# An encoder layer with a mixture of experts on one core: another form of the router, other weight buffers, a written order of the weight queue, and a last block by columns

## The chip, the cores and the metric

The kernel runs on one core of one Trainium2 chip. A core has five engines with a program of their own each: TensorE (PE: matmuls; PEld: its weight loads), VectorE (DVE), ScalarE (ACT), GpSimd (POOL) and SyncE (SP, which here only issues DMAs). Sixteen DMA engines move data between HBM and the core's SBUF. What is measured is the device time in microseconds (us) of one execution, as a median over runs.

## What is computed

One layer of a bidirectional encoder over 256 tokens of width 2048, in fp32, and a last norm:

```python
mod = silu(c) @ ada_w + ada_b                    # [1, 6*2048]
sh1, sc1, g1, sh2, sc2, g2 = split(mod, 6)
h = modulate(rmsnorm(x, norm1_g), sh1, sc1)
x = x + g1 * mixer(h, ...)                       # attention + FFT branches, gates, w_out
h = modulate(rmsnorm(x, norm2_g), sh2, sc2)
x = x + g2 * hier_moe(h, ...)                    # 4 groups x 8 experts, best group, top 2 in it
return rmsnorm(x, final_g)

# hier_moe: router, then SwiGLU experts of width 512
g_probs = softmax(h @ wg_r + bg_r)               # 4 groups
sel = (h @ we_r + be_r)[:, best group]           # 8 experts of it
weights = g_top_p * softmax(top2(sel))
y = sum over the two experts of weight * (silu(h @ w_gate[e]) * (h @ w_up[e])) @ w_down[e]
```

## The kernel before

The work is two long stages. In the **mixer stage** weights come as tiles of 128 x 1024 fp32 (512 KB) through `load` (L101 to L104): a tile is taken from the pool `wp`, which has NW = 8 buffers, and SP issues its DMA. Of each matmul tile ACT makes a rounded high part (`hi`, L107) and DVE the rest (`lo`, L108), so a buffer comes free when `lo` is done, and TensorE runs three matmuls (high by high, high by low, low by high) in place of one fp32 matmul: 24 of 256 columns or 12 of 512 columns per tile. Beside these run 192 tiles of the modulation matrix `ada_w`, which DVE alone multiplies (`dot`, L215, and `mac`, L223). SP's queue is in order: a load that waits for its buffer holds everything behind it. The order of SP's instructions up to the output projection is the scheduler's; in the projection's loop (L618 to L633) it is written out (`manual_schedule`).

The last part of the mixer is that projection (`mow`): four column blocks `cb` of 512, eight tiles each. Between its tiles stand `ada` tiles (`ada_some`), and quarters of the first five expert blocks (`early_some`, 20 loads of 512 KB into NA = 5 slots). The input is loaded again as `x1` (2 MB, L563); its place in SBUF is where gated sums of the mixer lay, so the load waits for the last gate addition on POOL (L543). After the last tile eight `ada` loads are issued (`late`). `residual` (L600 to L602) adds each column block to `x1` and makes its sum of squares on ACT; `router_part` transposes the block on TensorE, copies it on ACT, and accumulates the router's 36 logits in `plg` with the router's weights as the stationary operand: 4 matmuls with 256 moving columns. An fp32 matmul shows as two records. The part of block `cb` runs in the loop after five tiles of the next block; that of block 3 runs after the loop.

Then the **router chain**: sum of squares (L649), reciprocal root (L150 to L156), a copy of the logits to SBUF (`lgs`, L647), matmuls with a selection matrix that turn them to tokens by 36 (L116, `m<-cst,lgs`), `lg` (L656), best group and best two experts, ranks by a matmul with a triangular matrix, a gather matrix (`gt`, L742 and L744), and the gather itself (`ph`, `hq`), all on tiny tiles. The late `ada` tiles' `mac`s run on DVE ahead of it.

In the **expert stage** 192 blocks of 2 MB (`exw`, L727) stream from HBM: 8 quads of four experts, each with 16 gate/up blocks and 8 down blocks. A block takes a slot of SBUF and holds it until TensorE has used it. Slots 0 to 4 hold the early blocks, slots 5 and 6 (`wxb`) and 7 (`wx4`, used once, after which `x2` takes its place) can be loaded when the mixer's buffers are closed. After that NX = 7 slots go round. The last quad has a tail: `pd`, gate, `po`, residual, squares, then the norm's scale and four output DMAs.

Of the kernel before, what the change touches and what calls it, by code (L numbers as in the profile page):

```python
# [27 lines left out]
C_ID, C_LT, C_ONE, C_SELR, C_IOTA, C_DESC, C_THR, C_END = 0, 128, 256, 384, 420, 452, 484, 492  # L28
# [4 lines left out]
def const_table():  # L33
# [5 lines left out]
    for j in range(2):  # L39
        t[64 * j + np.arange(36), C_SELR + np.arange(36)] = 1  # L40
# [17 lines left out]
def build(tc, A, out, dbg=None):  # L58
# [15 lines left out]
    wp, _wp = pool("wp", "right", bufs=NW)  # L74
# [14 lines left out]
    def s4(shape, s, dt=F32):  # L89
        return r0.tile(shape, dt, tag="s4", bufs=6, name=nm(s))  # L90
# [74 lines left out]
    c16 = cp.tile([16, P], F32, name="c16")  # L165
    vec = cp.tile([P, P], F32, name="vec")
    vecT = cp.tile([P, P], F32, name="vecT")
    condT = cp.tile([P, KC], F32, name="condT")
    wr = cp.tile([P, KC, 36], F32, name="wr")
    rb = cp.tile([1, 36], F32, name="rb")  # L170
# [18 lines left out]

    condR = xp.tile([P, D], F32, name="condR")  # L190
    for i in range(2):
        crow = wp.tile([P, 1024], F32, tag="w", name=nm("crow"))
# [212 lines left out]
    for i, c in ((0, 1024), (2, 512)):  # L405
        fr = wp.tile([P, 1024], F32, tag="w", name=nm("fr"))
# [77 lines left out]
    def attention(half):  # L484
# [50 lines left out]
    _ra.close()  # L535
    mt, _mt = pool("mt", "right")
# [26 lines left out]
    nc.sync.dma_start(x1, A["x"])  # L563
# [32 lines left out]
    def residual(cb, acs):  # L596
        c = slice(512 * cb, 512 * cb + 512)
        for tb in range(2):
# [3 lines left out]
            nc.scalar.activation(tmp, x1[:, tb, c], AF.Square, accum_out=ss2[:, tb, cb:cb + 1])  # L602

    def router_part(cb):
        for pr in range(2):
            px = mps()
            for i in range(2):
                kc = 4 * cb + 2 * pr + i
                for tb in range(2):
                    nc.tensor.transpose(px[:, T * i + P * tb:T * i + P * tb + P],  # L610
                                        x1[:, tb, kc * P:kc * P + P], ident)
            xt2 = s4([P, 2, T], "x1t")
            nc.scalar.copy(xt2, px.rearrange("p (a b) -> p a b", a=2))
            for i in range(2):
                kc = 4 * cb + 2 * pr + i
                mm(plg[64 * i:64 * i + 36, 0:T], wra[:, kc, :], xt2[:, i, :], kc < 2, kc >= KC - 2)

    with tc.manual_schedule(engines={nc.sync.engine}):  # L618
        for cb in range(4):
            acs = acc_tiles()  # L620
            for s in range(8):
                n_part(load(A["mow"][cb, s]), acs, mhf, mlf, 2 * s, s == 0, s == 7)
                i = 8 * cb + s
                early_some(max(0, i - 5) * 4 * NA // 26 - max(0, i - 6) * 4 * NA // 26)
                ada_some((i + 1) * PACE // 32 - i * PACE // 32)
                if s == 4 and cb:
                    router_part(cb - 1)
                if s == 4 and cb == 1:

                    nc.scalar.activation(warm, ones[:, 0:1], AF.Sqrt)  # L630
            if cb == 3:
                late = [ada_load() for _ in range(len(ada_q))]
            residual(cb, acs)  # L633
    router_part(3)
    show("x1", x1)
    _mt.close()
    _wp.close()

    wxb, _wxb = pool("wxb", reuse_waits="tile")
    rt, _rt2 = pool("rt2", "right")  # L640
# [3 lines left out]
    lgs = rt.tile([P, T], F32, name="lgs")  # L644
    nc.gpsimd.memset(lgs, 0.0)
    for i in range(2):
        nc.vector.tensor_copy(lgs[64 * i:64 * i + 36, :], plg[64 * i:64 * i + 36, 0:T])  # L647
# [173 lines left out]
    for go in late:  # L821
        go()
# [172 lines left out]
```

## Time and profile before

| | us |
|---|---|
| median of three runs | 1601.78 (1601.13 to 1602.49) |
| the profiled execution, its own time | 1598.41 |
| its span (first to last instruction) | 1596.6 |
| mixer stage, about 15 to 640 of the span | 625 |
| router chain and gather, about 640 to 671 | 31 |
| expert stream, about 671 to 1581 | 910 |
| tail, about 1581 to 1597 | 16 |

Over the whole span PE is busy 77%, DVE 43%, ACT 22%, POOL 3%, and the DMA engines 95% in SP's queue. These are means over stages with different limits, so each stage has to be read by itself: first which engine is busy all the time in it, then which wait ends last where none is.

### The profile page before, as it was taken

The numbers are of one execution on the slowest core, as the hardware profiler recorded it, in microseconds if no ns is written. First come the engines' busy times: TensorE is split into PE (matmuls) and PEld (weight loads), VectorE is DVE, ScalarE is ACT, GpSimd is POOL, SyncE is SP. The second block draws the span as 40 slices with busy tenths as digits, with TensorE's granted clock in tenths as the row PEclk, the third lists the DMA queues.
The fourth block names the chain that finished last, engine by engine and source line by source line (L and its number), as shares of the span: only waits on it lengthen the run. The fifth ranks groups of instructions, "written<-read, shape, count | busy, mean of one in ns | idle before, by whom it ended". The sixth has DMA issues, their size and how long they took to land.

```text
span 1596.6 us, 20401 instructions
## 1 busy us (share of the span) xinstructions
PE 1233.2 (77%) x8430; PEld 745.9 (47%) x8430; DVE 679.3 (43%) x946; ACT 349.7 (22%) x535; POOL 43.6 (3%) x40
## 2 busy tenths in 40 slices
PE   4999999999999899679657567667567566556755
PEld 3989999999899777325112112112112112111111
DVE  6989999798887966603003002002002002002002
ACT  3543355444555343112000000000000000000002
POOL 0000000300002100000000000000000000000001
PEclk9999999999999999799889779789779889777878
DMA  9999999899997899699999999999999999999996
GB/s 360 389 337 339 352 359 365 273 328 369 329 346 267 318 409 380 261 427 426 427 426 427 428 427 426 427 426 427 426 427 428 427 427 426 417 427 426 425 428 280
DMA packets 89229, 616.27 MB, mean 386 GB/s; under 512 B 10037, under 2 KB 10341, under 8 KB 64937
## 3 DMA queue, kind: packets, MB, share of 16 engines
q1 hardware_dynamic: 87700, 611.10, 95.2%
q10 hardware_dynamic: 1252, 3.48, 0.6%
q8 instruction: 68, 1.11, 0.3%
q0 software_dynamic: 176, 0.31, 0.1%
q14 instruction: 33, 0.26, 0.0%
HBM read 611.71 MB, written 2.10 MB: 384 GB/s over the span
## 4 chain that ended last, share of the span: by engine, by line
DMA 47%; PE 38%; DVE 5%; issue 1%; ACT 1%; POOL 0%; DVEq 0%; POOLq 0%; ACTq 0%
DMA w<-exw 45%; PE acc L116 23%; PE pd L116 3%; PE m L116 2%; PE ph L116 2%; PE pg L116 2%; PE pu L116 2%; DMA w<-ada 2%; DVE lo L108 1%; DVE ada L223 1%; PE po L116 1%; PE at_u L116 1%; PE pr L116 0%; DVE t L600 0%; PE sp L116 0%
## 5 line engine op out<-in xcount | busy, mean ns | idle before, releaser
L116 PE MATMUL pg<-w,hq 128*32 128x512 f32 x1024 | 185.0, 777 | 217.0 <-DMA w<-exw 217.0
L108 DVE TENSOR_TENSOR lo<-w,hi 128x1024 fp32r<-128x1024 f32 x192 | 239.5, 1253 | 42.6 <-ACT hi L107 37.8
L107 ACT CAST hi<-w 128x1024 fp32r<-128x1024 f32 x192 | 200.8, 1051 | 229.2 <-PE acc L116 179.5
L790 DVE TENSOR_TENSOR act<-act,pu 128x512 f32<-128x512 f32 x8 | 5.5, 688 | 526.2 <-PE pu L116 526.2
L116 PE MATMUL acc<-hh,hi 128*128 128x256 f32 x768 | 212.1, 280 | 0.6 <-ACT hi L107 0.6
L116 PE MATMUL acc<-hl,hi 128*128 128x256 f32 x768 | 211.3, 278 | 0.0
L116 PE MATMUL acc<-hh,lo 128*128 128x256 f32 x768 | 205.7, 279 | 2.2 <-DVE lo L108 2.1
L116 PEld LDWEIGHTS pg<-w,hq 128*32 128x32 f32 x1024 | 25.0, 118 | 363.1 <-DMA w<-exw 345.3
L116 PE MATMUL pu<-w,hq 128*32 128x512 f32 x1024 | 190.0, 793 | 0.0
L223 DVE SCALAR_TENSOR_TENSOR ada<-w,condT,ada 128x1024 f32<-128x1024 f32 x124 | 162.1, 1314 | 13.1 <-DMA w<-ada 12.2
L116 PE MATMUL pd<-w,aT 128*32 128x512 f32 x1024 | 132.2, 630 | 37.0 <-DMA w<-exw 35.5
L116 PEld LDWEIGHTS acc<-hh,hi 128*128 128x128 f32 x768 | 145.3, 189 | 2.1 <-ACT hi L107 1.4
L116 PEld LDWEIGHTS acc<-hl,hi 128*128 128x128 f32 x768 | 145.1, 189 | 0.3 <-issue 0.2
L786 ACT ACTIVATE act<-pg 128x512 f32<-128x512 f32 x8 | 4.8, 597 | 637.3 <-PE pg L116 637.3
L116 PEld LDWEIGHTS acc<-hh,lo 128*128 128x128 f32 x768 | 141.2, 189 | 3.0 <-DVE lo L108 2.6
L116 PE MATMUL po<-yb,gwt 128*128 128x512 f32 (+1 forms) x132 | 75.0, 659 | 30.4 <-DVE yb L808 19.4
L116 PEld LDWEIGHTS pu<-w,hq 128*32 128x32 f32 x1024 | 43.0, 138 | 109.9 <-issue 108.2
L116 PEld LDWEIGHTS ph<-gt,x 128*128 128x128 f32 x512 | 65.2, 195 | 43.8 <-issue 25.6
L116 PEld LDWEIGHTS pd<-w,aT 128*32 128x32 f32 x1024 | 28.7, 112 | 114.7 <-issue 60.4
L215 DVE SCALAR_TENSOR_TENSOR w<-w,condR 128x1024 f32<-128x1024 f32 x64 | 77.7, 1219 | 9.1 <-ACT condR L197 7.4
L116 PE MATMUL ph<-gt,x 128*128 128x128 f32 x512 | 74.8, 288 | 7.1 <-ACT hq L756 3.5
L815 DVE TENSOR_TENSOR x<-x,po 128x512 f32<-128x512 f32 (+1 forms) x66 | 44.3, 671 | 79.8 <-PE po L116 79.8
(246 smaller groups left out, 1481.4 us busy)
## 6 DMA issues: line engine op xcount, KB each, us to landing
w<-exw SPq DMA_DIRECT2D x186, 2048.0 KB, 30.7
w<-ada SPq DMA_DIRECT2D x192, 512.0 KB, 5.8
w<-mixw SPq DMA_DIRECT2D x64, 512.0 KB, 5.6
w<-gatew SPq DMA_DIRECT2D x64, 512.0 KB, 5.4
w<-mow SPq DMA_DIRECT2D x32, 512.0 KB, 10.2
w<-exw SPq DMA_DIRECT2D x24, 512.0 KB, 10.2
w<-fow SPq DMA_DIRECT2D x16, 512.0 KB, 5.3
w<-now SPq DMA_DIRECT2D x16, 512.0 KB, 5.1
```

Source lines behind the costliest of these rows:

```text
L107: nc.scalar.copy(hi, src)
L108: nc.vector.tensor_tensor(lo, src, hi.bitcast(F32), op=OP.subtract)
L116: return nc.tensor.matmul(ps, lhsT, rhs, start=start, stop=stop, skip_group_check=True)
L215: nc.vector.scalar_tensor_tensor(w, w, 1.0, condR[:, 1024 * kh:1024 * kh + 1024], op0=OP.mult, op1=OP.mult, accum_out=dst)
L223: nc.vector.scalar_tensor_tensor(a, w, condT[:, kc:kc + 1], a, op0=OP.mult, op1=OP.add)
L786: nc.scalar.activation(at_[:, 0], pg, AF.Silu)
L790: nc.vector.tensor_tensor(at_[:, 1], at_[:, 0], pu, op=OP.mult)
L815: nc.vector.tensor_tensor(x2[:, tb, c], base[:, tb, c], po[:, 0:n], op=OP.add)
```

## The change

1. **Router chain.** `router_part` uses the transposed `x1` as the stationary operand and the 36 router columns as the moving one, so that logits come out as tokens by 36: 8 matmuls (16 records) per column block in place of 4 (8 records). The copies `lgs`, their memset, the selection matmuls and the selection matrix go. The square of the last half block is made on DVE. The late `ada` `mac`s, the group softmax, and the weights of the second choice stand behind the gather's last eviction (`issue_after`), as does the gather of the next quad.
2. **Buffers.** Work tiles of the mixer move to pools of their own (`r4`, `cq`) that are closed after it; the expert stage has small pools (`rt2`, `tp`). NX is 8, and `wx4` is a ninth slot. In the mixer two half-megabyte buffers (`wq`) are added to the eight until the attention's output projection begins.
3. **SP's order in the mixer** is written from the start of the weight stream to the end of `mow` (`written`), and stops before the expert loads. The `x1` load stands behind the fifth `mow` tile. The attention's bias loads (eight of 256 KB) are issued by POOL.
4. **Last block by columns.** The last two down blocks of the last quad are laid out on the host by 128 columns; they come as 2 x 1 MB and as 1 MB + 2 x 0.5 MB, and each column piece is closed with its own gate, residual and squares. The scale with the final gain is on POOL up to column 1792 (before: 1536), and one output DMA is issued by ACT.

The core of the diff:

```diff
+    wp, _wp = pool("wp", "right")
+    wq, _wq = pool("wq", "right")
+    rings = [(wp, i) for i in range(NW)] + [(wq, i) for i in range(NW, NW + NQX)]
...
+    def half(s):
+        p, i = rings.pop(0)
+        rings.append((p, i))
+        return p.tile([P, 1024], F32, tag=f"w{i}", bufs=1, name=nm(s))
+
     def load(src):
-        w = wp.tile([P, 1024], F32, tag="w", name=nm("w"))
+        w = half("w")
         nc.sync.dma_start(w, src)
         return w
...
+    written = ExitStack()
+    written.enter_context(tc.manual_schedule(engines={nc.sync.engine}))
...
-            nc.sync.dma_start(bt, A["rpb"][4 * half + i])
+            nc.gpsimd.dma_start(bt, A["rpb"][4 * half + i])
...
+    rings[:] = [r for r in rings if r[0] is wp]
+    _wq.close()
...
     x1 = x1p.tile([P, 2, D], F32, name="x1")
-    nc.sync.dma_start(x1, A["x"])
...
-            nc.scalar.activation(tmp, x1[:, tb, c], AF.Square, accum_out=ss2[:, tb, cb:cb + 1])
+            if cb == 3 and tb:
+                nc.vector.scalar_tensor_tensor(tmp, x1[:, tb, c], 1.0, x1[:, tb, c], op0=OP.mult, op1=OP.mult,
+                                               accum_out=ss2[:, tb, cb:cb + 1])
+            else:
+                nc.scalar.activation(tmp, x1[:, tb, c], AF.Square, accum_out=ss2[:, tb, cb:cb + 1])
...
     def router_part(cb):
+        px = [mps() for _ in range(2)]
...
-                mm(plg[64 * i:64 * i + 36, 0:T], wra[:, kc, :], xt2[:, i, :], kc < 2, kc >= KC - 2)
+                for tb in range(2):
+                    mm(plg[:, 36 * tb:36 * tb + 36], xt2[:, i, tb * P:tb * P + P], wra[:, kc, :],
+                       kc == 0 and tb == 0, kc == KC - 1)
-    with tc.manual_schedule(engines={nc.sync.engine}):
-        for cb in range(4):
...
+            i = 8 * cb + s
+            if i == 4:
+                nc.sync.dma_start(x1, A["x"])
...
+        residual(cb, acs)
+    written.close()
+    router_part(3)
...
-    lgs = rt.tile([P, T], F32, name="lgs")
-    nc.gpsimd.memset(lgs, 0.0)
-    for i in range(2):
-        nc.vector.tensor_copy(lgs[64 * i:64 * i + 36, :], plg[64 * i:64 * i + 36, 0:T])
...
-    pl = mps()
-    for tb in range(2):
-        mm(pl[:, 36 * tb:36 * tb + 36], lgs[:, tb * P:tb * P + P], cst[:, C_SELR:C_SELR + 36], True, True)
...
+            if q == NQ - 1 and cb == 3:
+                for k2 in range(2):
+                    w = get(A["exw"][q, KC + 2 * cb + k2], (2048, 4096) if tail is None or k2 == 0 else
+                            (2048, 3072, 4096))
+                    for i in range(2):
+                        c = slice(256 * k2 + 128 * i, 256 * k2 + 128 * i + 128)
...
+                        if k2:
+                            down(cb, c, pd, yb)
+                    if k2 == 0:
+                        down(cb, slice(0, 256), pd, yb)
...
     hg = gather(0, rk, 1)
+    behind, first_evict = ExitStack(), last_evict[0]
+    behind.enter_context(tc.issue_after(last_evict[0].ins))
     for go in late:
         go()
...
-        hg = gather(q + 1, rk, q % 2)
+        with tc.issue_after(first_evict.ins) if q == 0 else ExitStack():
+            hg = gather(q + 1, rk, q % 2)
...
-NW, NX, NA = 8, 7, 5
+NW, NQX, NX, NA = 8, 2, 8, 5
+LASTC = 1792
```

How the instructions stand is shown at three places. The first is SP's queue at the end of the mixer; before, three expert blocks (for slots 5 to 7) follow the late `ada` loads, and then comes the load of a count for the last branch.

```order
L103 DMA w_7030<-mow 128x1024
L572 DMA w_6297<-exw 128x1024
L103 DMA w_7049<-ada 128x1024
L103 DMA w_7052<-ada 128x1024
L103 DMA w_7054<-ada 128x1024
L103 DMA w_7056<-ada 128x1024
L103 DMA w_7058<-ada 128x1024
L103 DMA w_7060<-ada 128x1024
L103 DMA w_7062<-ada 128x1024
L103 DMA w_7064<-ada 128x1024
L103 DMA w_7066<-ada 128x1024
L727 DMA w_7327<-exw 128x4096
L727 DMA w_7337<-exw 128x4096
L727 DMA w_7347<-exw 128x4096
L869 TENSOR_LOAD nri
```

After the change the queue at this place reads as follows, where `w_7391` to `w_7431` are the second loads of slots 0 to 4 and `w_7351` to `w_7381` the first loads of slots 5 to 8:

```order
L111 DMA w_7084<-ada 128x1024
L111 DMA w_7086<-ada 128x1024
L111 DMA w_7088<-ada 128x1024
L746 DMA w_7391<-exw 128x4096
L746 DMA w_7401<-exw 128x4096
L746 DMA w_7411<-exw 128x4096
L746 DMA w_7421<-exw 128x4096
L746 DMA w_7431<-exw 128x4096
L746 DMA w_7351<-exw 128x4096
L746 DMA w_7361<-exw 128x4096
L746 DMA w_7371<-exw 128x4096
L746 DMA w_7381<-exw 128x4096
L913 TENSOR_LOAD nri
```

The first loads of slots 5 to 8 moved behind the five second loads of slots 0 to 4. Second is SP's queue at the `x1` load (`x_6285` before, `x_6297` after):

```order
L103 DMA w_6386<-mow 128x1024
L103 DMA w_6404<-mow 128x1024
L103 DMA w_6422<-ada 128x1024
L103 DMA w_6425<-mow 128x1024
L103 DMA w_6443<-mow 128x1024
L103 DMA w_6461<-ada 128x1024
L103 DMA w_6464<-mow 128x1024
L563 DMA x_6285<-x 128x4096
L572 DMA w_6293<-exw 128x1024
L103 DMA w_6493<-mow 128x1024
```

```order
L111 DMA w_6395<-mow 128x1024
L111 DMA w_6413<-mow 128x1024
L645 DMA x_6297<-x 128x4096
L111 DMA w_6432<-ada 128x1024
L111 DMA w_6435<-mow 128x1024
L111 DMA w_6453<-mow 128x1024
L111 DMA w_6471<-ada 128x1024
L111 DMA w_6474<-mow 128x1024
L584 DMA w_6304<-exw 128x1024
L111 DMA w_6503<-mow 128x1024
```

The `x1` load moved ahead of three `mow` and two `ada` loads. Third is DVE's program between the mixer's last `lo` and the router's logits, before:

```order
L600 TENSOR_TENSOR t_7068<-acc_6869,g1r_5907 128x512
L223 SCALAR_TENSOR_TENSOR ada_5950<-w_7052,condT,ada_5950 128x1024
L600 TENSOR_TENSOR t_7072<-acc_6870,g1r_5907 128x512
L601 TENSOR_TENSOR x_6285<-x_6285,t_7068 128x512
L223 SCALAR_TENSOR_TENSOR ada_5950<-w_7054,condT,ada_5950 128x1024
L601 TENSOR_TENSOR x_6285<-x_6285,t_7072 128x512
L223 SCALAR_TENSOR_TENSOR ada_5950<-w_7056,condT,ada_5950 128x1024
...
L223 SCALAR_TENSOR_TENSOR ada_5950<-w_7066,condT,ada_5950 128x1024
L649 TENSOR_REDUCE sst<-ss_6323 128x2
L150 TENSOR_SCALAR rv_7112<-sst 128x2
L647 COPY lgs<-plg 36x256 x2
L152 RECIPROCAL rr_7114<-rs_7113 128x2
```

and after:

```order
L612 TENSOR_TENSOR t_7090<-acc_6887,g1r_5919 128x512
L612 TENSOR_TENSOR t_7094<-acc_6888,g1r_5919 128x512
L613 TENSOR_TENSOR x_6297<-x_6297,t_7090 128x512
L613 TENSOR_TENSOR x_6297<-x_6297,t_7094 128x512
L615 SCALAR_TENSOR_TENSOR t_7094,ss_6334<-x_6297 128x512
L673 TENSOR_REDUCE sst<-ss_6334 128x2
L158 TENSOR_SCALAR rv_7139<-sst 128x2
L160 RECIPROCAL rr_7141<-rs_7140 128x2
...
L677 SCALAR_TENSOR_TENSOR lg<-plg,rr_7141,cbr 128x36 x2
```

The eight `mac`s of late `ada` tiles (L223 before, L234 after), which stood ahead of the sum of squares, are no longer there; they moved behind the gather, and one square was added.

## Rows read from the trace of the kernel before

**Rows 1.** Busy time by engine in stretches of the span; first line names the columns.

```profile
core 0: us, PE busy (x) PEld busy (x) DVE busy (x) ACT busy (x) POOL busy (x), PEclk, DMA share, GB/s
15.00:640.00 625.00, 595.54 (x4604) 550.17 (x4605) 542.26 (x638) 285.80 (x403) 33.50 (x25) 0.99 0.94 345
...
555.00:640.00 85.00, 82.05 (x377) 64.22 (x376) 53.45 (x51) 33.38 (x44) 0.00 (x0) 1.00 1.01 393
640.00:671.00 31.00, 15.29 (x80) 10.03 (x82) 23.83 (x75) 5.47 (x13) 1.05 (x3) 0.61 0.55 225
671.00:1581.00 910.00, 611.49 (x3730) 181.40 (x3722) 103.65 (x206) 48.60 (x101) 7.56 (x6) 0.85 1.00 425
```

**Rows 2.** The same columns, in steps of 5 us around the router chain.

```profile
645.00:650.00 5.00, 3.48 (x14) 1.68 (x14) 5.00 (x6) 1.90 (x4) 0.00 (x0) 0.50 1.00 426
...
655.00:660.00 5.00, 0.44 (x3) 0.30 (x2) 4.24 (x26) 0.41 (x2) 0.00 (x0) 0.50 0.23 98
...
670.00:675.00 5.00, 5.00 (x44) 2.45 (x46) 0.82 (x2) 0.91 (x2) 0.00 (x0) 1.00 0.85 303
```

**Rows 3.** Longest wait of PE, 15 to 280: line, releaser, us, times, longest.

```profile
PE px L348 <- DVE xt L342: 11.3, 1, 11.3
```

**Rows 4.** Timeline of SP's queue: start, us, line, what is loaded, count.

```profile
537.41 1.46 SPq L103 DMA_DIRECT2D w<-mow  x2
...
545.64 0.33 SPq L103 DMA_DIRECT2D w<-mow  x1
550.24 0.33 SPq L563 DMA_DIRECT2D x<-x  x1
```

**Rows 5.** Timeline of POOL: the last gate addition.

```profile
546.96 3.25 POOL L543 TENSOR_TENSOR g<-m,g 128x1024 f32<-128x1024 f32 x1 [11.86 <-DVE g L542]
```

**Rows 6.** Timeline of PE: `mow` matmuls, the second after a wait.

```profile
541.62 0.40 PE L116 MATMUL acc<-lo,mh 128*128 128x512 f32 x1
...
552.48 0.50 PE L116 MATMUL acc<-lo,mh 128*128 128x512 f32 x1 [1.07 <-DVE lo L108]
```

**Rows 7.** DMA issues: count, size, median us from issue to landing.

```profile
x<-x SPq DMA_DIRECT2D x1, 2048.0 KB, 7.7
```

**Rows 8.** Timeline of all engines, 640 to 666 (router chain and gather).

```profile
641.44 1.28 DVE L223 SCALAR_TENSOR_TENSOR ada<-w,condT,ada 128x1024 f32<-128x1024 f32 x1
...
645.03 0.68 DVE L601 TENSOR_TENSOR x<-x,t 128x512 f32<-128x512 f32 x1
645.63 7.26 DVE L223 SCALAR_TENSOR_TENSOR ada<-w,condT,ada 128x1024 f32<-128x1024 f32 x6
...
647.40 1.93 PE L116 MATMUL plg<-x1t,wr 128*36 128x256 f32 x8
...
653.00 0.16 DVE L649 TENSOR_REDUCE sst<-ss 128x2 f32<-128x8 f32 x1
...
654.40 1.04 PE L116 MATMUL m<-cst,lgs 128*128 128x36 f32 x4 [5.08 <-issue]
...
655.48 0.42 DVE L656 SCALAR_TENSOR_TENSOR lg<-m,rr,cbr 128x36 f32<-128x36 f32 x2 [0.30 <-PE m L116]
...
660.59 1.76 PE L116 MATMUL m<-ma,cst 128*128 128x32 f32 x10 [5.15 <-DVE w L833]
...
662.71 0.73 DVE L742 TENSOR_TENSOR gt<-rk,cst 128x128 f32<-128x128 f32 x3
...
665.95 0.63 PE L767 MATMUL pt<-cst,gt 128*128 128x128 f32 x2
```

**Rows 9.** Timeline of SP's queue: the first expert load behind the chain.

```profile
669.82 87.08 SPq L727 DMA_DIRECT2D w<-exw  x22
```

**Rows 10.** Timeline of PE in the mixer: a router part in the loop.

```profile
605.06 1.06 PE L116 MATMUL plg<-x1t,wr 128*36 128x256 f32 x8
```

**Rows 11.** Timeline of all engines in the tail.

```profile
1581.12 1.05 PE L116 MATMUL pd<-w,aT 128*32 128x512 f32 x4 [0.21 <-DMA w<-exw]
...
1586.16 0.16 DVE L897 TENSOR_REDUCE sst<-ss 128x2 f32<-128x10 f32 x1 [0.60 <-ACT sq L890]
...
1590.40 1.14 SPq L918 DMA_DIRECT2D out<-x  x1
```

More of the change, by code (lines that the diff above doesn't have):

```diff
@@ L89, in s4 @@
     def s4(shape, s, dt=F32):
-        return r0.tile(shape, dt, tag="s4", bufs=6, name=nm(s))
+        return r4.tile(shape, dt, tag="s4", bufs=6, name=nm(s))
     turn = [1]
@@ L405, in build @@
     for i, c in ((0, 1024), (2, 512)):
-        fr = wp.tile([P, 1024], F32, tag="w", name=nm("fr"))
+        fr = half("fr")
         nc.sync.dma_start(fr[:, 0:c], A["dft"][:, 512 * i:512 * i + c])
@@ L609, in router_part @@
                 for tb in range(2):
[L610 to L613, printed above, removed]
-            for i in range(2):
-                kc = 4 * cb + 2 * pr + i
-                mm(plg[64 * i:64 * i + 36, 0:T], wra[:, kc, :], xt2[:, i, :], kc < 2, kc >= KC - 2)
-    with tc.manual_schedule(engines={nc.sync.engine}):
-        for cb in range(4):
[L620 to L633, printed above, removed]
@@ new lines, in router_part @@
+                    mm(plg[:, 36 * tb:36 * tb + 36], xt2[:, i, tb * P:tb * P + P], wra[:, kc, :],
+                       kc == 0 and tb == 0, kc == KC - 1)
+    for cb in range(4):
+        acs = acc_tiles()
+        for s in range(8):
+            n_part(load(A["mow"][cb, s]), acs, mhf, mlf, 2 * s, s == 0, s == 7)
+            i = 8 * cb + s
+            if i == 4:
+                nc.sync.dma_start(x1, A["x"])
+            early_some(max(0, i - 5) * 4 * NA // 26 - max(0, i - 6) * 4 * NA // 26)
+            ada_some((i + 1) * PACE // 32 - i * PACE // 32)
+            if s == 4 and cb:
+                router_part(cb - 1)
+            if s == 4 and cb == 1:
+                nc.scalar.activation(warm, ones[:, 0:1], AF.Sqrt)
+        if cb == 3:
+            late = [ada_load() for _ in range(len(ada_q))]
+        residual(cb, acs)
@@ L634, in build, with temp @@
+    written.close()
     router_part(3)
     show("x1", x1)
-    _mt.close()
-    _wp.close()
+    for e in (_mt, _wp, _r4, _cq):
+        e.close()
+    rt, _rt2 = pool("rt2", reuse_waits="tile")
     wxb, _wxb = pool("wxb", reuse_waits="tile")
-    rt, _rt2 = pool("rt2", "right")
+    tp, _tp = pool("tp", "right", reuse_waits="tile")
+    def temp(shape, s, bufs=1):
+        return tp.tile(shape, F32, tag=s, bufs=bufs, name=nm(s))
     wx4, _wx4 = pool("wx4", "right", reuse_waits="tile")
-    lgs = rt.tile([P, T], F32, name="lgs")
@@ L716, in ring, with get @@
         todo, there = list(order) + list(once), list(there)
-        def get(src, parts=1):
+        def get(src, ends=(4096,)):
             if not todo:
@@ L724, in get @@
                 w = slot(i)
-                n = 4096 // parts
-                for i in range(parts):
-                    eng.dma_start(w[:, n * i:n * i + n], src[:, n * i:n * i + n])
+                for i, e in zip((0,) + ends, ends):
+                    eng.dma_start(w[:, i:e], src[:, i:e])
             return [w[:, 512 * j:512 * j + 512] for j in range(8)]
@@ L854, in build @@
     show("rk", rk)
+    behind.close()
     for q in range(NQ - 1):
@@ L885, in build, with tail @@
             nc.scalar.copy(fg[:, 1024 * j + 512 * i:1024 * j + 512 * i + 512], pr)
-    ss3 = rt.tile([P, 2, 5], F32, name="ss3")
-    def tail(x2, tb, i, c, gain):
+    ss3 = rt.tile([P, 2, 6], F32, name="ss3")
+    parts = [0, 0]
+    def tail(x2, tb, c):
         n = c.stop - c.start
-        nc.scalar.activation(s4([P, 512], "sq")[:, 0:n], x2[:, tb, c], AF.Square, accum_out=ss3[:, tb, i:i + 1])
-        if gain:
+        nc.scalar.activation(temp([P, 512], "sq")[:, 0:n], x2[:, tb, c], AF.Square,
+                             accum_out=ss3[:, tb, parts[tb]:parts[tb] + 1])
+        parts[tb] += 1
+        if c.start < LASTC:
             nc.gpsimd.tensor_tensor(x2[:, tb, c], x2[:, tb, c], fg[:, c], op=OP.mult)
@@ L911, in build @@
     scaled(nc.scalar, 0, c0)
[L912 removed]
+    nc.scalar.dma_start(out[:, 0, c0], x2[:, 0, c0])
     scaled(nc.vector, 1, c1)
```

94 lines of the change are left out of this document (52 added, 42 removed).

## The prediction

> **What bounds the kernel now.** I read the stretches of the span first, then the waits, then the timelines of the places that the change touches. From 15 to 640 us TensorE is busy 595.54 of 625 us at a granted clock of 0.99, while the DMA share is 0.94 [rows 1]: TensorE's pace bounds the mixer stage, and all that it doesn't work there is 29.5 us. The longest of its waits in the first half, 11.3 us, is for a transposition of the input [rows 3], and not for weights. In the output projection, 555 to 640, TensorE works 82.05 of 85 us and the DMA share is 1.01: there both limits stand side by side, and nothing that either of them loses comes back.
>
> From 671 to 1581 the DMA engines are full (share 1.00, 425 GB/s), and TensorE is not (611 of 910 us): expert bytes bound that stage. One block of 2.097 MB takes 2.097 / 425 = 4.93 us. Of 192 blocks five are loaded in the mixer and three in the router chain, so 184 remain for 910 us, 4.95 us each. I take 4.93.
>
> Between the two lies the router chain. The DMA share falls to 0.23 in 655 to 660, and is 0.85 in 670 to 675 [rows 2]: the DMA engines stop at about 655 + 0.23 x 5 = 656.2 and start at 675 - 0.85 x 5 = 670.8. They idle for 14.6 us because the next load needs slot 0, which comes free when the first expert block has been used; SP issues it at 669.82 [rows 9]. What counts of this chain is therefore two things: when slot 0 comes free, and how many blocks have landed by then.
>
> **The router chain, its length.** Before, the last half of `x1` is done at 645.71, the eight `mac`s occupy DVE until 652.9, and the sum of squares starts at 653.00 [rows 8]. Two more `mac`s of 1.28 us stand between the parts of the residual. After, none of them does. `x1` ends about 2 us earlier, near 643.7; its square on DVE, as long as the addition beside it (0.68), brings the sum to about 644.6. From the sum to `lg` it took 2.48 us (653.00 to 655.48), so the root would be there at about 647.1. TensorE is then the later one. Its last four transposes (two took 0.63 us) [rows 8] end near 644.8, and with the ACT copy behind them, which I put at 0.6 to 0.7 like the addition of the same 512 columns, the logits start at about 645.4. The trace has no matmul with `x1` stationary and 36 columns moving at the logits, so I bound it: the nearest rows are the selection matmuls, 4 records in 1.04 us (0.26 each), and the rank matmuls, 10 records in 1.76 (0.176), both of the same shape, 128 stationary columns and few moving ones, both at clock 0.50. Sixteen records take 2.8 to 4.2 us; I take 3.3, hence `lg` at 648.7 in place of 655.48: 6.8 us (6 to 8). Copies, memset and selection matmuls lie within that. Behind `lg` the work is the same as before, less half a `gt` group that stood in front (about 0.5 of 0.73) and two transposes that now stand behind the first block's work (0.63, I count 0.45). Slot 0 comes free about 7.75 us earlier, and the DMA engines start at about 663.0.
>
> **The router chain, its loads.** This is the largest term, and it has the other sign. Before, the first loads of slots 5 to 7 stand right behind the late `ada` loads and flow during the chain. After, SP's queue has the second loads of slots 0 to 4 there, and only then the first loads of slots 5 to 8. The second load of slot 0 waits for the first expert block to be used. SP's queue is in order, so four blocks whose places are free wait behind it, and nothing is loaded in the chain. The ninth slot cannot help either. At 663.0 there are 192 - 5 = 187 blocks to come in place of 184 at 670.8: 3 x 4.93 = 14.8 us more bytes, 7.75 us earlier start, so +7.0 us. With the ends of the chain's length and up to 2 us for `mac`s of late tiles that hold a place, +4 to +10. The late `mac`s (8 x 1.2 us) now end near 674, when DMA is still busy with five blocks (to 663 + 24.7 = 687.7), so they are hidden; with those five blocks first, they would only be seen if they came 14 us later. The group softmax and second weights, moved with them, are under the same cover. TensorE will wait for block 5 from about 667 to 692, but it has a third of its time over in this stage, so I count that at nothing; without that slack it would be 25 us.
>
> **The ring of eight.** It changes no byte of a stage whose DMA share is 1.00; at 425 GB/s against the 426 of a full stretch (645 to 650) [rows 2] there are at most 2 us to win. I count 0.
>
> **The `x1` load.** It waits for POOL's last gate addition, 546.96 + 3.25 = 550.21 [rows 5], and is issued at 550.24 [rows 4]. Before, SP stands there from 545.97, 4.3 us. After, it stands behind the fifth `mow` tile, from about 538.9 (537.41 + 1.46), 11.3 us, and behind it on the queue wait three `mow` and two `ada` tiles, 2.6 MB or 6.2 us of DMA, which before were issued during that time. What is late next is the sixth `mow` tile. TensorE has four matmuls of the first tile behind it at 541.62 [rows 6]; 8 + 4 x 12 more at 0.22 us (82.05 / 377) [rows 1] and the wait of 1.07 put the sixth at about 555. In the new queue it comes behind 2 MB of `x1` and one `ada` tile: 550.24 + 3.15 MB / 425 = 557.7, and up to 560.4 with the 2.8 us by which the `x1` load took longer than its bytes (7.7 in all) [rows 7]. With the split behind that, TensorE stalls 3 to 6 us; I take 4.6. None of it comes back where DMA and TensorE are both full.
>
> **The router's matmuls in the loop.** Three parts run between `mow` matmuls. Now a part takes 1.06 us [rows 10]. Sixteen records of 128 stationary columns at half of 0.176 to 0.26 us (the clock is full there) take 1.4 to 2.1 us; I add 0.75 for each, +2.2 (1 to 3).
>
> What a page makes of this: the Trainium skill, "TensorE: Matmul & The Clock Gate", section "Back-to-back issue gap", tables a lone matmul of 1 to 64 columns at about 25 ns, by its moving columns alone. By it a part would take 0.4 us and be cheaper than now. The rank matmuls above, seven times as long with 32 moving columns (at half clock), disagree. The result that the rule gives is a rival below.
>
> **Ten buffers, bias loads on POOL.** The part of the 29.5 us of waiting for weights is small; I found no wait of TensorE for a DMA in the list of its waits, only for `hi` and `lo`. Two more buffers ahead can take away some of these. I take -1.5 (-6, about a fifth of the 29.5, to +3, if bias loads from POOL come late to the attention's additions).
>
> **The tail.** From the last `pd` (1581.12) to the sum of squares (1586.16) it took 5.04 us [rows 11]. With the last piece 128 columns wide, the chain behind the last load has one gate, one `po` and one residual of half the width and one square less: I take -2.25 (-1 to -3). The outputs keep their bytes (2.1 MB, 4.9 us at 425 GB/s), which end the span; moved queues win nothing.
>
> **Sum.** +7.0 + 4.6 + 2.2 - 1.5 - 2.25 = +10.05. On the profiled execution's own 1598.41 that is 1608.5. The median of the runs, 1601.78, lies 3.4 above it; the forecast on that is 1611.8.
>
> **Rivals.**
> 1. The mixer pays for it, the other side. Buffers and the written order take away more than 10 of the 29.5 us that TensorE doesn't work up to 640. For it: an 11.3 us wait at one place, and the DMA share under 1 before 555. Against it: that wait is for DVE, and no wait for weights is on TensorE's list. From 11.5 us on it ends at no change; at 17 it gives 1601.78 + 10.05 - 15.5 = 1596.3. Chance 0.21, of which faster 0.15.
> 2. The stalled `x1` load costs its whole 6.2 us of DMA and more: 555 to 640 has a DMA share of 1.01, so late bytes push on to the last `mow` tile, and the three router parts with them. Some 6 us on top: 1618. Chance 0.12.
> 3. The short matmuls are bound by moving columns. Then three parts save 0.66 each in place of costing 0.75 (-4.2), and the chain waits for the root at 647.1 instead of TensorE (-1.6): 1606.0. Against it stand both rows of such matmuls. Chance 0.09. The page named above gives this.
> 4. The change doesn't do what its ninth slot says: that is the forecast itself. If the loads did flow in the chain, four blocks would land in it and 183 remain at 663.0: the gap term would be -4.9 - 7.75 = -12.7 and the sum -9.6. The order of SP's queue is fixed before the run, so I give it nothing.
>
> **How the numbers follow.** The forecast has 0.58, and its terms' ends reach from about 1604 to 1619. A measurement of this kernel can tell about 0.2%, 3.2 us, from no change: 1598.6 to 1605.0. Faster: 0.15 of rival 1. Same: 0.06 of rival 1, 0.05 of the forecast, 0.02 of rival 3, 0.13. Slower: 0.72. The range of 1601 to 1620 leaves out most of rival 1 and the top of rival 2.
>
> **What would show it.** In the new profile the DMA share should be near 0 for about 20 us once the late `ada` tiles have landed, and the first expert load behind the late `ada` loads should be issued when TensorE has used block 0. TensorE should wait about 25 us for block 5. SP should stand over 10 us at the `x1` load, with a wait of TensorE for `hi` some 10 us later. A mixer that ends before 640 would make the forecast wrong, as would expert loads that flow during the chain.

## The result and the profile after

The kernel after takes **1622.57 us** (median of 4 runs, 1620.76 to 1624.06), the kernel before beside it 1602.13 (1601.13 to 1606.46). The ratio is 1.0122, with an interval of 1.010 to 1.0143: slower, as forecast, but by 20.4 us where the sum said 10, and 2.6 above the range. The profiled execution took 1622.06 with a span of 1620.3, 23.7 more than before.

The first view is busy time by stage; it answers to [rows 1].

```profile
core 0: us, PE busy (x) PEld busy (x) DVE busy (x) ACT busy (x) POOL busy (x), PEclk, DMA share, GB/s
15.00:640.00 625.00, 589.13 (x4521) 547.96 (x4521) 530.21 (x626) 276.91 (x393) 44.77 (x33) 0.98 0.88 334
...
640.00:671.00 31.00, 27.26 (x139) 22.26 (x137) 20.00 (x34) 10.42 (x16) 0.00 (x0) 0.97 0.69 243
671.00:1581.00 910.00, 613.99 (x3690) 184.18 (x3694) 117.86 (x254) 47.75 (x97) 0.92 (x3) 0.83 0.99 422
```

TensorE is still busy 94% of the time to 640, but has done 4521 matmul records there and not 4604, and from 640 to 671 it is still in the mixer at a clock of 0.97, where before it did a few small matmuls at 0.61. So the mixer ends later. Its last `acc` matmul starts at 663.8 and not at 641.3, +22.5. A gauge on the way is POOL's last gate addition, 546.96 before [rows 5]:

```profile
559.12 5.57 POOL L556 TENSOR_TENSOR g<-m,g 128x1024 f32<-128x1024 f32 x1 [10.49 <-DVE g L555]
```

It starts 12.2 us later, before any change of the output projection can act, and takes 5.57 in place of 3.25 us. (Four trials below leave the mixer of after as it is up to this point, and start it at 561.1 to 561.6: one trace is good to some 2.5 us here.) The next loss is at the `x1` load, in SP's queue ([rows 4]):

```profile
550.87 1.52 SPq L111 DMA_DIRECT2D w<-mow  x2
564.72 0.33 SPq L645 DMA_DIRECT2D x<-x  x1
565.14 0.38 SPq L111 DMA_DIRECT2D w<-ada  x1
565.61 1.03 SPq L111 DMA_DIRECT2D w<-mow  x2
```

SP stands from 552.39 to 564.72, 12.3 us (forecast: 11.3). TensorE's timeline shows the answer 11 us later, and the stretch that holds it shows the clock:

```profile
570.23 0.39 PE L124 MATMUL acc<-lo,mh 128*128 128x512 f32 x1
576.13 0.80 PE L124 MATMUL acc<-hi,mh 128*128 128x512 f32 x1 [5.51 <-ACT hi L115]
```

```profile
575.00:580.00 5.00, 3.87 (x9) 3.10 (x10) 3.78 (x4) 3.15 (x3) 0.00 (x0) 0.50 1.02 384
```

A wait of 5.51 us for `hi`, and behind it a granted clock of 0.50, the lower level, at which the 3.87 us of work do what 1.9 would at the full clock (an estimate).

Then the chain (timeline, all engines; [rows 8] and [rows 9]) and its stretches ([rows 2]):

```profile
666.98 0.16 DVE L673 TENSOR_REDUCE sst<-ss 128x2 f32<-128x8 f32 x1
...
667.36 1.98 PE L124 MATMUL plg<-wr,x1t 128*128 128x36 f32 x16 [0.51 <-ACT x1t L631]
...
669.37 0.42 DVE L677 SCALAR_TENSOR_TENSOR lg<-plg,rr,cbr 128x36 f32<-128x36 f32 x2 [0.49 <-PE plg L124]
...
683.90 13.37 SPq L746 DMA_DIRECT2D w<-exw  x6
...
700.51 2.47 DVE L234 SCALAR_TENSOR_TENSOR ada<-w,condT,ada 128x1024 f32<-128x1024 f32 x2
```

```profile
660.00:665.00 5.00, 4.21 (x19) 3.16 (x17) 1.45 (x3) 0.00 (x0) 0.00 (x0) 1.00 0.64 238
665.00:670.00 5.00, 3.14 (x24) 2.70 (x24) 3.56 (x14) 1.90 (x5) 0.00 (x0) 0.94 0.00 0
670.00:675.00 5.00, 0.52 (x3) 0.55 (x3) 3.73 (x18) 0.00 (x0) 0.00 (x0) 0.50 0.00 0
...
685.00:690.00 5.00, 5.00 (x43) 2.00 (x37) 0.41 (x1) 0.88 (x2) 0.00 (x0) 1.00 0.85 334
```

`lg` stands 5.6 us behind the mixer's last matmul, where before it was 14.2 (641.3 to 655.48). The first expert load is issued at 683.90, 14.1 later than before: +22.5 of the mixer less 8.4 of the chain. The DMA engines idle from 660 + 0.64 x 5 = 663.2 to 690 - 0.85 x 5 = 685.75, 22.5 us in place of 14.6 (but for shares of 0.02 and 0.16 in the two stretches left out). The tail (timeline; [rows 11]):

```profile
1605.77 1.08 PE L124 MATMUL pd<-w,aT 128*32 128x128 f32 x32
...
1609.04 0.17 DVE L945 TENSOR_REDUCE sst<-ss 128x2 f32<-128x12 f32 x1 [0.74 <-ACT sq L936]
...
1612.93 0.93 SPq L966 DMA_DIRECT2D out<-x  x1
```

The last expert bytes land at 1604.50 (before 1581.08, +23.4), and from there to the end it takes 15.8 us (before 15.5).

### The profile page after: what moved, and what is told of

It is laid out like the page before. It is cut to its first block, busy times and chain, and to the rows that moved or that the text cites. A ratio compares the mean times of both kernels' runs of the same rounds, so it can differ in the third digit from the quotient of the medians.

```text
span 1620.3 us, 20576 instructions
## 1 busy us (share of the span) xinstructions
PE 1259.0 (78%) x8558; PEld 765.8 (47%) x8558; DVE 681.5 (42%) x949; ACT 349.6 (22%) x537; POOL 55.7 (3%) x49
## 4 chain that ended last, share of the span: by engine, by line
DMA 48%; PE 38%; DVE 4%; issue 2%; ACT 1%; POOL 0%; SPq 0%; DVEq 0%; ACTq 0%; POOLq 0%
DMA w<-exw 46%; PE acc L124 24%; PE m L124 3%; PE pd L124 3%; PE pg L124 2%; PE pu L124 2%; PE ph L124 1%; PE po L124 1%; DVE lo L116 1%; DVE ada L234 1%; DMA w<-ada 1%; DMA w<-now 0%; PE plg L124 0%; PE sp L124 0%; ACT hi L115 0%
## 5 line engine op out<-in xcount | busy, mean ns | idle before, releaser
L234 DVE SCALAR_TENSOR_TENSOR ada<-w,condT,ada 128x1024 f32<-128x1024 f32 x124 | 162.8, 1319 | 18.0 <-DMA w<-ada 17.9
L124 PE MATMUL pd<-w,aT 128*32 128x512 f32 (+1 forms) x1120 | 130.7, 587 | 37.8 <-DMA w<-exw 37.0
L124 PE MATMUL po<-yb,gwt 128*128 128x512 f32 (+2 forms) x136 | 74.3, 637 | 31.0 <-DVE yb L819 20.1
L124 PEld LDWEIGHTS pu<-w,hq 128*32 128x32 f32 x1024 | 42.4, 141 | 115.8 <-issue 114.7
L124 PEld LDWEIGHTS ph<-gt,x 128*128 128x128 f32 x512 | 65.8, 196 | 47.4 <-issue 22.3
L826 DVE TENSOR_TENSOR x<-x,po 128x512 f32<-128x512 f32 (+2 forms) x68 | 44.4, 655 | 81.7 <-PE po L124 81.6
```

Source lines behind the costliest of these rows:

```text
L124: return nc.tensor.matmul(ps, lhsT, rhs, start=start, stop=stop, skip_group_check=True)
L234: nc.vector.scalar_tensor_tensor(a, w, condT[:, kc:kc + 1], a, op0=OP.mult, op1=OP.add)
L826: nc.vector.tensor_tensor(x2[:, tb, o], base[:, tb, o], po[:, 0:n], op=OP.add)
```

## The experiments

A difference to after, here and below, is one of medians. The kernel before ran beside each trial again, with medians of 1602.85 (32 bytes, `x1`, two blocks), 1602.07 (64 bytes, 128 and 32, `mac`s, old tail) and 1599.55 (160 bytes, bias loads, all three), so the ratio beside each time is to its own runs of before; where this shifts a reading, the text says so.

The main question is the 12.2 us ahead of the projection. TensorE's waits up to the gate addition are a small part of them: those on its list sum to 31.4 us, and to 28.6 before. What differs more is the matmuls themselves. Worked out from the start times in the traces, the mixer's 256-column records start 116.9 ns after one another in the mean where they follow each other closely (steps of 100 to 130 ns), and 114.2 before. Some 3450 such steps of 2.66 ns more make 9.2 us, and with the 2.8 of the waits 12.0. In the timeline of TensorE, before (first and last of 13 rows, 12 steps of 113 ns) and after (8 rows, 7 steps of 117 ns):

```profile
206.78 0.28 PE L116 MATMUL acc<-hh,hi 128*128 128x256 f32 x1
...
208.14 0.28 PE L116 MATMUL at_u<-hh,lo 128*128 128x256 f32 x1
```

```profile
232.04 0.28 PE L124 MATMUL acc<-hh,hi 128*128 128x256 f32 x1
...
232.86 0.28 PE L124 MATMUL acc<-hl,hi 128*128 128x256 f32 x1
```

The granted clock is 1.00 in both stretches. The change moves the tiles in SBUF, so their places were the first suspect. "Pace" below is that mean; `hh` (with `hl`) is the moving tile of most of these matmuls, and `hi` (with `lo`) the stationary one.

**Before, with 32 unused bytes in SBUF.** A tile of 8 words is allocated ahead of the mixer's pools; the program's instructions and their order stay the same.

```diff
+    padp, _padp = pool("padp", "right")
+    padt = padp.tile([P, 8], F32, name="padt")
     r0, _r0 = pool("r0", "right")
...
```

> The kernel before with the same 32 bytes left unused at the top of SBUF, nothing else changed, so that hi and lo lie 32 bytes off the moving operand modulo 64, as in the changed kernel. Theory A: its matmuls of 256 columns go from 113 to about 117 ns and the time rises by about 10 us, to about 1612. Theory B: no change, 1602.

1610.02 us, 1.005 (1.0033 to 1.0066). Pace 118.3; the gate addition starts at 558.29, 11.3 later than before, and 7.2 us of it reach the time. In the traces every engine runs the same instructions in the same order as in before, so nothing but the place of the tiles on the right side of SBUF is changed. In TensorE's and POOL's timelines (12 steps of 118 ns):

```profile
205.75 0.28 PE L118 MATMUL acc<-hh,hi 128*128 128x256 f32 x1
...
207.17 0.28 PE L118 MATMUL acc<-hh,lo 128*128 128x256 f32 x1
```

```profile
558.29 3.25 POOL L545 TENSOR_TENSOR g<-m,g 128x1024 f32<-128x1024 f32 x1 [11.86 <-DVE g L544]
```

**After, with the same 32 bytes.**

> The changed kernel with 32 bytes left unused at the top of SBUF, so that the work buffers hi and lo (and the weight buffers) lie 64 bytes off the moving operand hh modulo 128, as in the kernel before; the order of every engine's instructions is that of the changed kernel. Theory A (the place of the operands sets the matmuls' pace, 113 ns before and 117 ns after for 256 columns): the pace returns to about 113 ns, the mixer ends about 10 us earlier, time about 1612. Theory B (the written order, the bias loads or the new buffers delay the mixer): the pace stays at 117 ns, time within 2 us of the changed kernel, about 1622.

1625.92, 1.0142 (1.0125 to 1.0159), pace 117.65. A shift back is no remedy; the form of the theory that let 32 bytes decide fell.

**Before, with 64 bytes.** The same edit with 16 words.

> The kernel before with 64 bytes in place of 32 left unused at the top of SBUF. Theory A (what counts is whether stationary and moving operand agree modulo 64): the pace is 113 ns again and the time 1602, where 32 bytes gave 118 ns and 1610. Theory B (any shift disturbs it): 118 ns, about 1610.

1615.66, 1.0087 (1.0064 to 1.0110). Pace 119.8, the gate addition at 562.84. The rule "equal modulo 64 bytes is as good" fell, and the reading that places set the pace stood. In its timeline (6 steps of 120 ns):

```profile
205.83 0.28 PE L118 MATMUL m<-hh,hi 128*128 128x256 f32 x1
...
206.55 0.28 PE L118 MATMUL acc<-hh,hi 128*128 128x256 f32 x1
```

**After, with 128 bytes on the left and 32 on the right,** so that `hh` and `hi` both lie where they lay before, modulo 4096 bytes.

```diff
+    padl, _padl = pool("padl")
+    padlt = padl.tile([P, 32], F32, name="padlt")
     cp, _cp = pool("cp")
+    padr, _padr = pool("padr", "right")
+    padrt = padr.tile([P, 8], F32, name="padrt")
...
```

> The changed kernel with 128 bytes left unused at the bottom of SBUF and 32 at its top, so that hh and hi both lie where they lay before modulo 4096; the instructions and their order are those of the changed kernel. Theory A (the operands' places modulo 4096 set the matmuls' pace): 113 ns in the mixer again, about 1612. Theory B (the pace follows from something else, such as the order of the work around): 117 to 118 ns as with 32 bytes alone, 1622 to 1626.

1622.19, 1.0126 (1.0099 to 1.0152), which neither theory had: no gain in the time, though the pace is 115.0 and the mixer's last `acc` matmul comes 3.9 earlier (659.9). The stretch from 720 to 1550 shows where it went, here of before, of after and of this kernel, one row each:

```profile
720.00:1550.00 830.00, 547.70 (x3306) 160.89 (x3298) 93.10 (x184) 38.11 (x78) 0.00 (x0) 0.84 1.01 426
```

```profile
720.00:1550.00 830.00, 561.47 (x3394) 162.69 (x3390) 93.09 (x184) 36.45 (x76) 0.00 (x0) 0.84 1.01 429
```

```profile
720.00:1550.00 830.00, 556.58 (x3386) 166.51 (x3378) 93.23 (x184) 36.41 (x76) 0.00 (x0) 0.85 1.01 427
```

The same bytes, with slots 128 bytes further on, stream at 427 and not 429 GB/s, and 0.5% of some 920 us is about the 4 us. The eight other kernels made from after leave the left side where it is, and all stream at 429 in this stretch.

**After, with 160 bytes on the right only,** which makes the distance between `hh` and the first `hi` buffer 64 bytes modulo 256, as before, and leaves the slots on the left where they were.

```diff
+    padr, _padr = pool("padr", "right")
+    padrt = padr.tile([P, 40], F32, name="padrt")
     r0, _r0 = pool("r0", "right")
...
```

> The changed kernel with 160 bytes left unused at the top of SBUF, nothing else: hi then lies 64 bytes off hh modulo 256, as in the kernel before and in the run with 128 and 32 bytes, while the expert slots stay where the changed kernel has them. Theory A (this distance modulo 256 decides): 113 ns for most matmuls of 256 columns, the mixer ends 4 to 10 us earlier, about 1614. Theory B (the distance modulo 256 is not the rule): 117 ns or more, 1620 to 1627.

1617.21, 1.0112 (1.0097 to 1.0128), 5.4 less than after; against its own runs of before only 2.8 less, with intervals that overlap, so the times alone don't show the gain. The trace does, in the mixer: pace 114.7, a gate addition 6.4 earlier than in after, in the timeline 10 steps of 113 ns, and the stream keeps 429 GB/s:

```profile
205.76 0.28 PE L126 MATMUL m<-hl,hi 128*128 128x256 f32 x1
...
206.89 0.28 PE L126 MATMUL acc<-hh,hi 128*128 128x256 f32 x1
```

In this table the distance between `hh` and the first `hi` buffer is worked out from the sizes of the pools' tiles.

| kernel | distance mod 256, bytes | pace, ns | gate addition starts |
|---|---|---|---|
| before | 64 | 114.2 | 546.96 |
| before + 32 | 32 | 118.3 | 558.29 |
| before + 64 | 0 | 119.8 | 562.84 |
| after | 224 | 116.9 | 559.12 |
| after + 32 | 192 | 117.7 | 562.20 |
| after + 128 and 32 | 64 | 115.0 | 555.86 |
| after + 160 | 64 | 114.7 | 552.76 |

All three kernels at 64 are quicker than the four others. The pace belongs to the places and not to the run: the four trials below that move no tile of the mixer (`x1`, `mac`s, two blocks, old tail) have 116.9 to 117.0, as after has. That after + 160 still starts its gate addition 5.8 later than before is mostly waits: 1.6 are pace, and 3.4 are TensorE's waits (32.0 in place of 28.6). What stays open is the rule. All tiles on the right move together here, and kernels at 64 also have stretches at 116 to 118 ns with the same tiles (before, from 265 to 280 us), so the distance of these two is not the whole of it; why the place matters is not shown.

**The `x1` load behind the eighth tile.**

```diff
-            if i == 4:
+            if i == 7:
```

> The changed kernel with the x1 load behind the eighth output projection tile, where it stood before, in place of behind the fifth. Theory A (its wait holds back five loads that the projection needs): SP stands under 6 us there in place of 12.3, TensorE's wait of 5.7 us for hi goes, and the time falls by 6 to 10 us, to about 1614. Theory B (POOL's late gate addition delays the mixer by itself, the queue only shows it): 0 to 2 us.

1614.85, 1.0076 (1.0059 to 1.0093), 7.7 less than after (8.4 against its own runs of before). The queue stands 3.1 us (563.92 to 566.98) and the wait for `hi` is gone:

```profile
563.59 0.33 SPq L111 DMA_DIRECT2D w<-mow  x1
566.98 0.33 SPq L645 DMA_DIRECT2D x<-x  x1
```

From the gate addition to the last `acc` matmul it is 94.3 us before, 104.7 after and 96.8 here. Of the 2.5 that stay over before, 1.3 are the three longer router parts.

**Late `mac`s ahead of the chain again.** With this alone the scheduler also puts the first loads of slots 5 to 8 ahead of the second loads of slots 0 to 4.

```diff
+    for go in late:
+        go()
     sst = rt.tile([P, 2], F32, name="sst")
...
     behind.enter_context(tc.issue_after(last_evict[0].ins))
-    for go in late:
-        go()
```

> The changed kernel with the eight multiplications of late ada tiles ahead of the sum of squares again, as before; the scheduler then puts the first loads of slots 5 to 8 ahead of the second loads of slots 0 to 4. Theory A (an empty queue in the chain is the largest loss of the expert stage): the chain is 8 to 10 us longer, but four blocks of 4.9 us land in it, so the time falls by 9 to 12 us, to about 1612. Theory B (the length of the chain is what counts): it rises by 8 to 10 us, to about 1631.

1613.43, 1.0067 (1.0045 to 1.0088), 9.2 less than after. Its chain is longer, `lg` at 679.16, and yet it wins, since the blocks flow as the `mac`s end (stretches, and SP's queue). The edit changes two things at once, the `mac`s' place and the queue's order, and the gain is that of both:

```profile
670.00:675.00 5.00, 4.17 (x20) 3.90 (x20) 5.00 (x7) 1.07 (x2) 0.00 (x0) 0.59 0.57 242
675.00:680.00 5.00, 0.12 (x1) 0.00 (x0) 4.66 (x14) 0.20 (x1) 0.00 (x0) 0.50 0.20 39
680.00:685.00 5.00, 0.72 (x4) 0.76 (x4) 3.57 (x17) 0.00 (x0) 0.00 (x0) 0.50 0.94 387
```

```profile
666.28 60.47 SPq L748 DMA_DIRECT2D w<-exw  x17
```

**Blocks 5 and 6 loaded ahead, the `mac`s left late.** Block 5 goes to slot 5, block 6 to the ninth slot (index 8), both ahead of the chain; the rounds over the slots are renumbered to fit.

```diff
+    for k, (p, i) in enumerate(((wxb, NA), (wx4, NX))):
+        first.append(p.tile([P, 4096], F32, tag=f"w{i}", bufs=1, name=nm("w")))
+        first_load = nc.sync.dma_start(first[k], A["exw"][0, NA + k])
...
```

> The changed kernel with the loads of blocks 5 and 6 put ahead of the second loads of slots 0 to 4 in SP's queue, into slots 5 and 8, which don't wait for the late ada tiles; slots 6 and 7 follow behind the second loads of 0 to 4. Theory A (the order of the queue leaves the DMA engines idle in the router chain): two blocks of 4.9 us land in the chain, the stream ends 9 to 10 us earlier, time about 1613. Theory B (the DMA engines are not what bounds the expert stage's start): under 2 us.

1640.89, 1.0236 (1.0219 to 1.0253), 18 more than after; a miss for the theory that these places are free. SP's queue and DVE:

```profile
666.51 42.16 SPq L673 DMA_DIRECT2D w<-exw  x2
708.76 15.45 SPq L750 DMA_DIRECT2D w<-exw  x9
```

```profile
702.70 2.47 DVE L234 SCALAR_TENSOR_TENSOR ada<-w,condT,ada 128x1024 f32<-128x1024 f32 x2
...
705.73 2.46 DVE L234 SCALAR_TENSOR_TENSOR ada<-w,condT,ada 128x1024 f32<-128x1024 f32 x2
```

The second of the two loads stands until 708, because the ninth slot lies over the last mixer buffer, which a late `ada` tile holds until its `mac`. The trace of after agrees: there the first load of slot 5 is issued at 696.84, right behind the second loads of slots 0 to 4, and those of slots 6 to 8 only when the last late `mac` has ended (DVE, and SP's queue):

```profile
709.19 2.45 DVE L234 SCALAR_TENSOR_TENSOR ada<-w,condT,ada 128x1024 f32<-128x1024 f32 x2
```

```profile
711.67 1.28 SPq L746 DMA_DIRECT2D w<-exw  x3
```

So with the `mac`s late most of these places aren't free: for slots 6 to 8 a short chain and loads in the chain exclude each other here. Slot 5 ends below the eight buffers and could be loaded; that it alone would win one block is read from the places and wasn't run.

**The old tail.** The kernel after with the last block by halves as before (and its scale split at 1536).

```diff
-            if q == NQ - 1 and cb == 3:
+            if False:
...
-LASTC = 1792
+LASTC = 1536
```

> The changed kernel with the last block as before (four loads of 512 KB, two pieces of 256 columns, gain on POOL up to column 1536); the order of the output loads' queues is kept. Theory A (the column pieces win nothing, because TensorE takes a piece only when the piece before it has gone through DVE): within 1 us of the changed kernel, 1622. Theory B (they win the 2.25 us that were forecast): 1625.

1623.36, 1.0133 (1.0109 to 1.0156), 0.8 over after with intervals that overlap: by the medians the columns win 1 us, which is not clear of the noise.

**Bias loads on SP again.**

```diff
-            nc.gpsimd.dma_start(bt, A["rpb"][4 * half + i])
+            nc.sync.dma_start(bt, A["rpb"][4 * half + i])
```

> The changed kernel with the eight bias loads issued by SP again, where they stood before in its order. Theory A (they cost and win nothing, since the attention's additions have slack): within 2 us of 1622. Theory B (loads issued by POOL come late and stall the attention): 2 to 5 us less.

1632.78, 1.0208 (1.0193 to 1.0224), 10 *more* than after (12.8 against its own runs of before), a miss for both theories. The attention's stretch of after, of this kernel, SP's queue in this kernel, and TensorE's waits in it (us in total, times, longest) that after doesn't have:

```profile
280.00:460.00 180.00, 178.14 (x1508) 162.50 (x1507) 152.46 (x164) 85.97 (x157) 27.76 (x27) 1.00 0.87 314
```

```profile
280.00:460.00 180.00, 171.97 (x1461) 158.55 (x1461) 144.24 (x157) 81.93 (x150) 20.46 (x19) 0.97 0.77 296
```

```profile
323.92 19.55 SPq L507 DMA_DIRECT2D bias<-rpb  x4
...
405.05 22.61 SPq L507 DMA_DIRECT2D bias<-rpb  x4
```

```profile
PE sp L124 <- DVE sb L516: 2.7, 3, 1.0
PE m L527 <- DVE sb L524: 1.9, 2, 1.1
```

In the written order four bias loads stand together on SP for some 20 us, and the weights behind them wait (DMA share 0.77 in place of 0.87); TensorE is busy 6.2 us less of the same 180, at a clock of 0.97. So the move to POOL is worth some 10 us to a queue in that order; in the kernel before, whose scheduler orders the loads, it is not shown to be worth anything.

**All three remedies in one:** 160 bytes, `x1` behind the eighth tile, late `mac`s ahead.

> The changed kernel with three edits together: 160 bytes unused at the top of SBUF, the x1 load behind the eighth tile, and the late multiplications ahead of the chain with four blocks in it. Theory A (pace, x1 wait and queue order are separate losses that add up): -7.7 from x1, -9.2 from the order, -4 to -10 from the pace, 1596 to 1602, faster than the kernel before or the same. Theory B (they overlap, DMA bound): 1606 or more.

1598.56 (1596.37 to 1600.50) against 1599.55 of before (1598.44 to 1605.82) beside it: 0.9986 (0.9976 to 0.9996). The three alone win 5.4, 7.7 and 9.2, in sum 22.3; together they win 24.0 (each against its own runs of before: 2.8, 8.4 and 9.1, in sum 20.3, and together 21.4). So the three gains nearly add up, and together they take back the whole difference. What is left of the change is about even with the kernel before: 0.14% quicker, less than the 0.2% that the forecast called a difference. That is a balance and not a mixer as quick as before: its last `acc` matmul starts at 649.67, still 8.4 later than before, and the expert stream runs at 429 and not 426 GB/s.

## Why the prediction was right and wrong

| term | forecast, us | trace, us |
|---|---|---|
| mixer up to the gates (buffers, bias loads) | -1.5 | +12.2 |
| `x1` load | +4.6 | +9.0 (7.7 in the time) |
| router parts in the loop | +2.2 | +1.3 |
| chain, length | -7.75 | -8.4 |
| blocks no longer loaded in it | +14.8 | +9.3 |
| tail | -2.25 | +0.3 |
| sum | +10.05 | +23.7 (span), +20.4 (medians) |

**The step that failed** is the term "Ten buffers, bias loads on POOL", -1.5, measured at +12.2. It priced waits only, with ends of -6 and +3, and put a change of TensorE's own pace at nothing without giving a reason. The runs showed in its place that the pace changes: 2.66 ns more for each 256-column matmul make 9.2 of the 12.2 us, and in the kernel before the same instructions in the same order, on tiles shifted by 32 bytes, cost 7.2 us more. Neither the diff nor a list of waits shows it; but the forecast put the stage down to TensorE's pace, busy 595.54 of 625 us, and the change gave the tiles of that stage new places. The waits that the term did price went the other way too, 2.8 us longer. Rival 1 was right that the mixer decides, and wrong on the sign: its wins from buffers and order were not seen; by the trial with the bias loads on SP, moving them to POOL only paid for the written order.

This term alone misses by 13.7 us, as much as the whole sum (23.7 for 10.05). The other five miss by +4.4, -0.9, -0.65, -5.5 and +2.55, which cancel to -0.1; that the rest of the sum came out is luck.

**The `x1` load** was the right mechanism, mis-sized by 3 to 4 us, for two reasons. POOL's addition took 5.57 us and not the 3.25 of [rows 5]. DVE's timeline says why; after, and then before:

```profile
558.90 1.27 DVE L234 SCALAR_TENSOR_TENSOR ada<-w,condT,ada 128x1024 f32<-128x1024 f32 x1
560.09 2.35 DVE L116 TENSOR_TENSOR lo<-w,hi 128x1024 fp32r<-128x1024 f32 x2
```

```profile
546.73 1.22 DVE L108 TENSOR_TENSOR lo<-w,hi 128x1024 fp32r<-128x1024 f32 x1
547.86 3.43 DVE L223 SCALAR_TENSOR_TENSOR ada<-w,condT,ada 128x1024 f32<-128x1024 f32 x1
```

After, three DVE instructions run to 562.44, and POOL ends 2.25 us behind them (564.69). Before, one runs to 547.95, POOL ends 2.26 behind it (550.21), and the `mac`, 1.28 elsewhere, takes 3.43 and ends 1.1 behind POOL. One stands while the other works. The Trainium skill, "SBUF — State Buffer", section "SBUF: two separate sides", has such a rule for a DVE instruction with two operands in SBUF against a GpSimd one that reads SBUF: whichever starts first has the shared pair of ports for the whole instruction, and the other waits. The rows of before agree; those of after agree in that POOL stands, but there DVE went on through three instructions before POOL had its turn, which the rule for one instruction does not say. The second reason is the clock of 0.50 behind the wait, worth some 2 us by the row above (an estimate), which the forecast left out. Rival 2, 6 us on top, comes near the size for another reason than it gave.

**The chain's length** was right: -8.4 for -7.75. The logits' 16 records took 1.98 us, below the 2.8 to 4.2 forecast, for a reason seen in the rows: TensorE came from the mixer at a clock of 0.94, and the 0.50 of the rows used as bounds did not hold. On the rank and selection matmuls' 0.176 to 0.26 that clock gives 0.094 to 0.138 each, and 0.124 was measured. Rival 3 therefore falls. By the 25 ns that the Trainium skill, "TensorE: Matmul & The Clock Gate", section "Back-to-back issue gap", tables for a lone matmul of so few columns, 16 records would take 0.4 us (an estimate); here, where each record has its own weight load, the trace has five times that. The loop's parts cost less than forecast on the same scale (+1.3 for +2.2), but cost.

**The loads in the chain** were right in sign and place: the DMA share is 0.00 from 665 to 675, and SP's first load behind the late `ada` tiles waits for block 0. Three more blocks are 14.8 us; of these 5.5 came back, in a stream of 429 GB/s in place of 426 (0.7% of 911 us is 6.4). The forecast gave the ring of eight "at most 2 us"; the shift by 128 bytes shows that the places of the slots move that rate, so whether the ring or the places won it stays open. The stated reason was half right. "Four blocks whose places are free" was wrong for three of the four: in after slots 6 to 8 are loaded only behind the last late `mac`, and in the trial with two blocks ahead the ninth slot's place was held by a late tile, 42 us of standing on SP. The forecast's allowance for that was 2 us.

**The tail** was wrong in sign. TensorE runs the pieces in turn (`pd`, a wait for `yb`, `po`, the next `pd`), so the last `pd` starts 1.27 us behind the last landing (1604.50) in place of 0.04. The sum of squares stands 3.27 behind that `pd` in place of 5.04 [rows 11], so 0.5 is saved there and not 2.25. From that sum to the end of the span it then takes 11.3 us in place of 10.4, though the last output is issued 3.9 behind it in place of 4.2: the outputs land later, for a reason that no run here shows. The old tail in the new kernel agrees that little is in it: 0.8 us.

**What would show it.** The DMA idle of about 20 us (22.5), SP's 10 us at `x1` (12.3) and TensorE's wait about 10 us later (11) were there. The wait of 25 us for block 5 was not: TensorE had the early blocks and the next gather until 713, with 10.8 us of waiting for DVE's gather matrices, which stood behind the late `mac`s (6.5 and 4.3; these ended at 711.64, where the forecast had them end near 674), and its longest wait for a block was 3.6. So the `mac`s were not hidden from TensorE, but from the end, since the stream bounds there. No end of the mixer before 640, and no loads in the chain.

## What to carry to other kernels

Where TensorE's pace bounds a stage, read the start-to-start time of one shape in both traces before looking for waits, and treat every change of the pools as a possible change of that pace: a few unused bytes ahead of the pools are a cheap experiment. Ahead of shortening a chain, list which tiles hold the places that the next loads need, and what frees them: moving that work behind the chain moves the loads behind it too. An in-order queue that is written by hand has to be read at each load that waits for an engine, with all that stands behind it.

## What the runs showed of the hardware

- Start-to-start time of one matmul shape (128 stationary, 256 moving columns, granted clock 1.00) went from 114.2 to 118.3 and 119.8 ns in the mean when the same program's tiles on the right side of SBUF moved by 32 and 64 bytes; steps of 113, 117 and 120 ns stand in the timelines.
- The same expert stream ran at 429 GB/s in after and in eight kernels made from it, and at 427 with its slots 128 bytes further on; before it was 426.
- A POOL addition of 128 x 1024 took 2.25 us behind the last DVE instruction that it met, and 5.57 in all where three of these ran on; a `mac`, 1.28 us elsewhere, took 3.43 beside one.
- Behind a TensorE wait of 5.51 us the granted clock was 0.50 in the next stretch of 5 us.
